# A residual load moved to a second queue, and the last stores rearranged, in a 3x3 convolution with residual add

## Chip, cores, metric

One core of one Trainium2 chip (trn2). The metric is device time in microseconds (us), lower is better. A run counts as slow when it is over 1.5% above the fastest of its kernel. One profile is one execution: sizes read from a single profile are sizes of that execution.

## Reference

```python
# x: 16 x 64 x 64 x 64, weight: 64 x 64 x 3 x 3, residual: 16 x 64 x 64 x 64, all float32
x_pad = np.pad(x, ((0, 0), (0, 0), (1, 1), (1, 1)), mode='constant')
for b, co, ci, kh, kw in ...:          # five loops
    output[b, co] += weight[co, ci, kh, kw] * x_pad[b, ci, kh:kh+h, kw:kw+w]
return (output + residual).astype(np.float32)
```

x and the residual are read once (16.8 MB each) and the output is written once (16.8 MB). With the weights that is 50.48 MB.

## The kernel before

Two images stand side by side on the 128 partitions (64 channels each) and are called a pair. There are 8 pairs. Per image, ScalarE casts x to bf16 into a padded tile, TensorE does 6 groups of 4 matmuls, and VectorE adds the result from PSUM to the residual, in place in `ro`. SyncE issues every load and store. `xr` holds three pairs of x, `ro` all eight pairs.

```python
RES = (slice(0, 1), slice(1, 2), slice(2, 4), slice(4, 6), slice(6, 8))   # residual loads, in pairs

def load_x(p):
    return nc.sync.dma_start(out=xr[p % NXR][:, :], in_=x_bc[128 * p : 128 * p + 128, :]).then_inc(s_x[p % NXR], 16)
def load_ro(i):
    if i >= 2:
        nc.sync.wait_ge(s_r[i % 2], 16 * (i // 2))
    nc.sync.dma_start(out=ro[:, RES[i], :], in_=res_bc[:, RES[i], :]).then_inc(s_r[i % 2], 16)
def store(pairs):
    return nc.sync.dma_start(out=out_bc[:, pairs, :], in_=ro[:, pairs, :])

# SyncE's program
for p in range(NPAIR):
    if p >= NXR:
        nc.sync.wait_ge(s_half, 2 * (p - NXR) + 3)     # buffer read, ScalarE's next cast done
    if p == 0:
        to_the_front(load_x(p))                        # ahead of the opening barrier
        nc.sync.dma_start(out=wraw[:, :], in_=w_rows[:, :]).then_inc(s_w, 16)
    else:
        load_x(p)
    if p in (0, 1, 3, 5, 7):
        load_ro((p + 1) // 2)
for k in range(NEARLY):                                # NEARLY = 3: pairs 0-1, 2-3, 4-5
    nc.sync.wait_ge(s_add, 4 * k + 5)
    store(slice(2 * k, 2 * k + 2)).then_inc(s_out, 16)
# ... ScalarE, VectorE and TensorE programs cut ...
for p in range(2 * NEARLY, NPAIR):                     # after all engines are done: pairs 6 and 7
    store(slice(p, p + 1))
```

Of the kernel before, what the change touches and what calls it, by code (L numbers as in the profile page):

```python
# [15 lines left out]
def kernel(  # L16
# [7 lines left out]
    nc = tc.nc  # L24
# [6 lines left out]
    NPIX = H * W  # L31
    NPAIR = B // 2
# [3 lines left out]
    NXR = 3  # L36
    NXP = 4
    NZERO = 4 + 2 * NXP
    NEARLY = 3
    RES = (slice(0, 1), slice(1, 2), slice(2, 4), slice(4, 6), slice(6, 8))  # L40

    res_bc = residual.rearrange("(p b) c h w -> (b c) p (h w)", b=2)
    out_bc = out.rearrange("(p b) c h w -> (b c) p (h w)", b=2)
# [7 lines left out]
    ro = pool.tile([128, NPAIR, NPIX], FP32)  # L51
# [10 lines left out]
    s_r = [sem(f"s_r{i}") for i in range(2)]  # L62
    s_out = sem("s_out")
# [5 lines left out]
    s_add = sem("s_add")  # L69

    def load_x(p):
        return nc.sync.dma_start(out=xr[p % NXR][:, :], in_=x_bc[128 * p : 128 * p + 128, :]).then_inc(s_x[p % NXR], 16)

    def load_ro(i):
        if i >= 2:
            nc.sync.wait_ge(s_r[i % 2], 16 * (i // 2))
        nc.sync.dma_start(out=ro[:, RES[i], :], in_=res_bc[:, RES[i], :]).then_inc(s_r[i % 2], 16)

    def store(pairs):
        return nc.sync.dma_start(out=out_bc[:, pairs, :], in_=ro[:, pairs, :])  # L80

    def matmul(out_, lhsT, rhs, start, stop, ldweights):

# [18 lines left out]
    def to_the_front(dma):  # L102



        def fixed(ap):
            t = ap.bass_ap.tensor.name
            return mybir.PhysicalAccessPattern(
                ap=ap.ap, offset=ap.bass_ap.offset, dtype=ap.dtype, memref=t, memsetref=t + "_set", bass_ap=ap.bass_ap
            )  # L110

        front = nc.main_func.blocks[0].instructions
        here = nc.cur_bb.bb.instructions
        ins = here.pop()
        assert ins.name == dma.ins.name
        at = next(
            i for i, e in enumerate(front) if e.engine == ins.engine and isinstance(e, mybir.InstDrain)
        )
        front.insert(at, copy.replace(ins, ins=[fixed(a) for a in ins.ins], outs=[fixed(a) for a in ins.outs]))
# [5 lines left out]
    def weight_block(h, half, d, par, kh):  # L125

        at = 64 * half + 32 * h
        return dict(out=wl[at : at + 32, d, :, par, :], in_=tp[0:32, kh, 0:384].rearrange("p (kw co h) -> p kw co h", kw=3, h=2)[:, :, :, h])

    with tc.tile_critical(no_gpsimd_drain=True):  # L130

        for p in range(NPAIR):
            if p >= NXR:

                nc.sync.wait_ge(s_half, 2 * (p - NXR) + 3)
            if p == 0:
                to_the_front(load_x(p))
                nc.sync.dma_start(out=wraw[:, :], in_=w_rows[:, :]).then_inc(s_w, 16)
            else:
                load_x(p)  # L140
            if p in (0, 1, 3, 5, 7):
                load_ro((p + 1) // 2)
        for k in range(NEARLY):
            nc.sync.wait_ge(s_add, 4 * k + 5)
            store(slice(2 * k, 2 * k + 2)).then_inc(s_out, 16)


        nc.gpsimd.memset(ident[:, :], 0.0).then_inc(s_id, 1)  # L148
# [2 lines left out]
            out=ident[:, :],  # L151
            in_=ident[:, :],
# [11 lines left out]
        nc.gpsimd.memset(wl[64:128, 1, :, 0, :], 0.0).then_inc(s_id, 1)  # L164


        for n in range(B):
            p, im = divmod(n, 2)
            hp = slice(64 * im, 64 * im + 64)
            x4 = xr[p % NXR].rearrange("q (j two w) -> q j two w", two=2, w=W)  # L170
            t = xp[n % NXP]
            if im == 0:
                nc.scalar.wait_ge(s_x[p % NXR], 16 * (p // NXR + 1))
            i = nc.scalar.copy(out=t[64:128, 0:J, :], in_=x4[hp, :, 0, :])  # L174
            i.then_inc(s_half, 1)
            if n >= NXP:
                i._wait_ge(s_conv, n - NXP + 1)
            nc.scalar.copy(out=t[0:64, 1 : J + 1, :], in_=x4[hp, :, 1, :]).then_inc(s_pack, 1)  # L178
            if n == 0:
                nc.scalar.wait_ge(s_id, NZERO + 1)  # L180
                for b in blocks[4:]:
                    for h in range(2):
                        i = nc.scalar.copy(**weight_block(h, *b))  # L183
                i.then_inc(s_id, 1)
# [3 lines left out]
        for k, b in enumerate(blocks[:4]):  # L188
            for h in range(2):
                i = nc.vector.tensor_copy(**weight_block(h, *b))  # L190
# [3 lines left out]
        for n in range(B):  # L194
            p, im = divmod(n, 2)
# [3 lines left out]
            if im == 0:  # L199
                i = next(i for i, pairs in enumerate(RES) if p < pairs.stop)  # L200
                nc.vector.wait_ge(s_r[i % 2], 16 * (i // 2 + 1))
            for par in range(2):
                i = nc.vector.tensor_tensor(  # L203
                    out=o4[hp, :, par, :], in0=psj[64 * par : 64 * par + 64, :, :], in1=o4[hp, :, par, :], op=ADD
                )
# [9 lines left out]
        for t in range(9):  # L215
            i = nc.tensor.transpose(  # L216
                out=tp[0:32, t // 3, 128 * (t % 3) : 128 * (t % 3) + 128], in_=wraw3[:, :, t], identity=ident[:, :]
            )
# [19 lines left out]
                m.then_inc(s_conv, 1)  # L238


    for p in range(2 * NEARLY, NPAIR):
        store(slice(p, p + 1))
    with tc.tile_critical(sync_engine=mybir.EngineType.Pool, no_gpsimd_drain=True):
        nc.gpsimd.wait_ge(s_out, 16 * NEARLY)
        tc.free_semaphores([s_w, *s_x, *s_r, s_out, s_id, s_half, s_pack, s_bank, s_conv, s_add])


# [28 lines left out]
```

## Time and profile before

| | kernel before |
|---|---|
| time, median (4 runs in the first comparison) | 122.81 us (122.63 to 122.95) |
| span of the profiled run | 120.8 us (122.68 us measured) |
| bytes moved, mean rate | 50.48 MB, 418 GB/s |
| first cast of x / first convolution / end of the last add | 7.79 / 13.78 / 104.28 us |
| last data packet ends | 119.6 us |

Two of the costliest groups of the page follow: the line and engine, what it writes and reads, the count, then busy time and mean ns of one, then the idle time of the engine just before them with what ended most of it.

```profile
L203 DVE TENSOR_TENSOR ro<-ps,ro 64x2048 f32<-64x2048 f32 x32 | 73.2, 2289 | 17.7 <-PE ps L87 17.2
...
L174 ACT CAST xp<-xr 64x2048 bf16<-64x2048 f32 x16 | 30.3, 1896 | 18.3 <-DMA xr<-in_x_dram 17.2
```

Both engines have slack: VectorE waits 17.7 us, almost wholly for TensorE, and ScalarE 18.3 us, almost wholly for x. Neither wait is what a reader should attack, because the DMA queue is full all the time (its packets took 98.5% of the 16 engines' span). The prediction below shows the lines for that.

Two quantities run through this document. They are worked out from the trace's record of single DMA packets (one packet is one row: 16 KB took 0.611 us in the middle of every run here, in the kernel before 2985 of 3072 rows; 8 KB is counted as half of that, 0.306). The **head** is the time that packets starting in the first 6 us took above those durations, summed and divided by 16 engines. In the profile before, the head is 1.04 us. The trace does not name a packet's engine. Each transfer of 64 rows or more leaves 16 packets of 4 bytes behind its rows. They are taken here as one per engine, and their times as where the transfer ends on each engine.

### The profile page before, as it was taken

What the parts mean: (1) busy time and instruction counts of PE and PEld (TensorE: products, weight loads), DVE (VectorE), ACT (ScalarE), POOL (GpSimd) and SP (SyncE); (2) the same over time, 40 slices, a digit from 0 to 9 for tenths busy, and PEclk for the clock granted to TensorE, in tenths of its full rate; (3) what the DMA queues carried; (4) which work ended last, traced back from release to release, by engine and by line L of the source; (5) the groups of instructions that cost most, each with busy time, mean ns of one, the idle gap of its engine ahead of it and who ended that gap; (6) DMA issues with size and microseconds to landing.
All of it is one profiled execution on the core that took longest, in us unless ns stands there. A gap on an engine that the chain in (4) does not pass through costs nothing.

```text
span 120.8 us, 734 instructions
## 1 busy us (share of the span) xinstructions
PE 87.9 (73%) x393; PEld 10.7 (9%) x105; DVE 76.0 (63%) x40; ACT 63.1 (52%) x37; POOL 2.4 (2%) x16
## 2 busy tenths in 40 slices
PE   0024499999999999999999999999999990000000
PEld 0011001101010011011111111011111100000000
DVE  0005400789898988989879898988989879500000
ACT  4049959948999923999960999883000000000000
POOL 5200000000000000000000000000000000000000
PEclk9999999999999999999999999999999999855555
DMA  7999999999999999999999999999999999999994
GB/s 168 428 428 428 428 428 434 428 434 434 428 434 434 434 428 434 434 434 434 434 434 423 423 428 434 423 412 434 434 434 434 423 434 434 434 428 434 434 434 174
DMA packets 3504, 50.48 MB, mean 418 GB/s; under 512 B 304, under 2 KB 432, under 8 KB 432
## 3 DMA queue, kind: packets, MB, share of 16 engines
q1 hardware_dynamic: 3504, 50.48, 98.5%
HBM read 33.70 MB, written 16.78 MB: 418 GB/s over the span
## 4 chain that ended last, share of the span: by engine, by line
PE 71%; DVEq 2%; DVE 2%; issue 0%
PE ps L87 53%; PE ps L86 18%; DVEq L130 2%; DVE ro L203 2%
## 5 line engine op out<-in xcount | busy, mean ns | idle before, releaser
L203 DVE TENSOR_TENSOR ro<-ps,ro 64x2048 f32<-64x2048 f32 x32 | 73.2, 2289 | 17.7 <-PE ps L87 17.2
L87 PE MATMUL ps<-xp,wl 128*128 128x504 bf16 (+1 forms) x288 | 80.0, 388 | 0.0
L86 PE MATMUL ps<-xp,wl 128*128 128x504 bf16 (+1 forms) x96 | 37.4, 389 | 3.4 <-PEq L224 3.4
L174 ACT CAST xp<-xr 64x2048 bf16<-64x2048 f32 x16 | 30.3, 1896 | 18.3 <-DMA xr<-in_x_dram 17.2
L178 ACT CAST xp<-xr 64x2048 bf16<-64x2048 f32 x16 | 30.4, 1897 | 0.4
L86 PEld LDWEIGHTS ps<-xp,wl 128*128 128x128 bf16 x96 | 9.5, 99 | 79.1 <-issue 79.1
L190 DVE CAST wl<-ps 32x192 bf16<-32x192 f32 x8 | 2.8, 348 | 10.6 <-PE ps L216 10.5
L216 PE MATMUL ps<-ident,wraw 128*32 128x128 f32 x9 | 2.1, 413 | 8.3 <-DMA wraw<-in_weight_dram 8.3
L216 PEld LDWEIGHTS ps<-ident,wraw 128*32 128x32 f32 x9 | 1.2, 137 | 8.7 <-issue 8.2
L174 ACT ACT_TABLE_LOAD x1 | 1.3, 1283 | 1.0 <-SPq L130 1.0
L183 ACT CAST wl<-ps 32x192 bf16<-32x192 f32 x4 | 1.2, 306 | 0.0
L162 POOL MEMSET xp<- 64x64 bf16 x4 | 0.6, 147 | 0.2
L161 POOL MEMSET xp<- 64x64 bf16 x4 | 0.6, 145 | 0.2
L150 POOL TENSOR_SCALAR_AFFINE_SELECT ident<-ident 128x128 f32<-128x128 f32 x1 | 0.3, 294 | 0.2 <-POOL ident L148 0.2
L164 POOL MEMSET wl<- 64x192 bf16 x1 | 0.3, 253 | 0.1
L163 POOL MEMSET wl<- 64x192 bf16 x1 | 0.3, 252 | 0.1
L148 POOL MEMSET ident<- 128x128 f32 x1 | 0.2, 205 | 0.6 <-SPq L130 0.6
L260 POOL MEMSET const-bfloat16-1.0<- 128x1 bf16 x1 | 0.1, 112 | 0.0
L260 POOL MEMSET const-uint8-127<- 128x1 uint8 x1 | 0.1, 112 | 0.0
L260 POOL MEMSET const-float32-0.0<- 128x1 f32 x1 | 0.1, 105 | 0.2 <-issue 0.2
L260 POOL MEMSET const-float32-1.0<- 128x1 f32 x1 | 0.1, 109 | 0.0
## 6 DMA issues: line engine op xcount, KB each, us to landing
xr<-in_x_dram SPq DMA_DIRECT2D x8, 2048.0 KB, 15.3
ro<-in_residual_dram SPq DMA_DIRECT2D x3, 4096.0 KB, 24.0
out_dram<-ro SPq DMA_DIRECT2D x3, 4096.0 KB, 33.2
ro<-in_residual_dram SPq DMA_DIRECT2D x2, 2048.0 KB, 15.9
out_dram<-ro SPq DMA_DIRECT2D x2, 2048.0 KB, 12.8
wraw<-in_weight_dram SPq DMA_DIRECT2D x1, 144.0 KB, 7.1
```

What stands on the lines that cost most here:

```text
L86: return e.matmul(out=out_, lhsT=lhsT, rhs=rhs, start=start, stop=stop, skip_group_check=True)
L87: return e.add_instruction(mybir.InstMatmult(name=nc.get_next_instruction_name(), engine=PE, ins=[e.lower_ap(rhs), e.lower_ap(lhsT)], outs ...
L130: with tc.tile_critical(no_gpsimd_drain=True):
L161: nc.gpsimd.memset(t[0:64, 0, :], 0.0).then_inc(s_id, 1)
L162: nc.gpsimd.memset(t[64:128, J, :], 0.0).then_inc(s_id, 1)
L174: i = nc.scalar.copy(out=t[64:128, 0:J, :], in_=x4[hp, :, 0, :])
L178: nc.scalar.copy(out=t[0:64, 1 : J + 1, :], in_=x4[hp, :, 1, :]).then_inc(s_pack, 1)
L183: i = nc.scalar.copy(**weight_block(h, *b))
L190: i = nc.vector.tensor_copy(**weight_block(h, *b))
L203: i = nc.vector.tensor_tensor(out=o4[hp, :, par, :], in0=psj[64 * par : 64 * par + 64, :, :], in1=o4[hp, :, par, :], op=ADD)
L216: i = nc.tensor.transpose(out=tp[0:32, t // 3, 128 * (t % 3) : 128 * (t % 3) + 128], in_=wraw3[:, :, t], identity=ident[:, :])
L260: nc = _bacc.Bacc("TRN2", target_bir_lowering=False, num_devices=1)
```

## The change

The intent: start the first residual load at once on ScalarE's own queue instead of third on SyncE's, so that the DMA engines have more to do from the start, and leave fewer bytes for after the last add: pair 6 is stored as soon as it is ready, and pair 7 in two halves.

```diff
-    NEARLY = 3
+    EARLY = (slice(0, 2), slice(2, 4), slice(4, 6), slice(6, 7))
-    def load_ro(i):
+    def load_ro(i, e):                     # body: nc.sync becomes e, and the dma is returned
-    def store(pairs):
-        return nc.sync.dma_start(out=out_bc[:, pairs, :], in_=ro[:, pairs, :])
+    def store(pairs, cols=slice(0, NPIX)):
+        return nc.sync.dma_start(out=out_bc[:, pairs, cols], in_=ro[:, pairs, cols])
-            if p in (0, 1, 3, 5, 7):
-                load_ro((p + 1) // 2)
-        for k in range(NEARLY):
-            nc.sync.wait_ge(s_add, 4 * k + 5)
-            store(slice(2 * k, 2 * k + 2)).then_inc(s_out, 16)
+            if p in (1, 3, 5, 7):
+                load_ro((p + 1) // 2, nc.sync)
+        for pairs in EARLY:
+            nc.sync.wait_ge(s_add, 2 * pairs.stop + 1)
+            store(pairs).then_inc(s_out, 16)
+        to_the_front(load_ro(0, nc.scalar))          # ahead of ScalarE's opening barrier
-    for p in range(2 * NEARLY, NPAIR):
-        store(slice(p, p + 1))
+    for h in range(2):
+        store(slice(NPAIR - 1, NPAIR), slice(NPIX // 2 * h, NPIX // 2 * (h + 1)))
-        nc.gpsimd.wait_ge(s_out, 16 * NEARLY)
+        nc.gpsimd.wait_ge(s_out, 16 * len(EARLY))
```

More of the change, by code (lines that the diff above doesn't have):

```diff
@@ L72, in load_x @@
         return nc.sync.dma_start(out=xr[p % NXR][:, :], in_=x_bc[128 * p : 128 * p + 128, :]).then_inc(s_x[p % NXR], 16)
-    def load_ro(i):
+    def load_ro(i, e):
         if i >= 2:
-            nc.sync.wait_ge(s_r[i % 2], 16 * (i // 2))
-        nc.sync.dma_start(out=ro[:, RES[i], :], in_=res_bc[:, RES[i], :]).then_inc(s_r[i % 2], 16)
-    def store(pairs):
-        return nc.sync.dma_start(out=out_bc[:, pairs, :], in_=ro[:, pairs, :])
+            e.wait_ge(s_r[i % 2], 16 * (i // 2))
+        return e.dma_start(out=ro[:, RES[i], :], in_=res_bc[:, RES[i], :]).then_inc(s_r[i % 2], 16)
+    def store(pairs, cols=slice(0, NPIX)):
+        return nc.sync.dma_start(out=out_bc[:, pairs, cols], in_=ro[:, pairs, cols])
     def matmul(out_, lhsT, rhs, start, stop, ldweights):
```

## The prediction

> **What bounds the kernel now.** I read the page first, for the row of DMA rates, then the chain of waits, then SyncE's own timeline and the short stretches at both ends.
>
> ```profile
> span 120.8 us, 734 instructions
> DMA  7999999999999999999999999999999999999994
> GB/s 168 428 428 428 428 428 434 428 434 434 428 434 434 434 428 434 434 434 434 434 434 423 423 428 434 423 412 434 434 434 434 423 434 434 434 428 434 434 434 174
> DMA packets 3504, 50.48 MB, mean 418 GB/s; under 512 B 304, under 2 KB 432, under 8 KB 432
> PE 71%; DVEq 2%; DVE 2%; issue 0%
> ```
>
> The span is cut into 40 slices of 3.02 us. Apart from the first and last slice, the 16 DMA engines are busy in all of them at 412 to 434 GB/s. The chain that ended last names TensorE (71%), but a chain is followed through instructions, and the bytes still waiting in a DMA queue are not instructions. VectorE's last add ends at 104.28 us, yet the span ends at 120.8: the 16 us after it are stores draining. So the bound is bytes: 50.48 MB at 430 GB/s is 117.4 us, plus a head and a tail. The only other way to lose time is to let the queue run empty.
>
> The stretches at the ends (columns: length, busy PE, PEld, DVE, ACT, POOL, PE clock, DMA share, GB/s):
>
> ```profile
> 0.50:1.00 0.50, 0.00 (x0) 0.00 (x0) 0.00 (x0) 0.04 (x1) 0.00 (x1) 1.00 0.00 0
> 1.00:1.50 0.50, 0.00 (x0) 0.00 (x0) 0.00 (x0) 0.50 (x1) 0.27 (x2) 1.00 2.87 524
> 1.50:2.00 0.50, 0.00 (x0) 0.00 (x0) 0.00 (x0) 0.50 (x1) 0.39 (x3) 1.00 0.38 66
> 2.00:2.50 0.50, 0.00 (x0) 0.00 (x0) 0.00 (x0) 0.24 (x1) 0.39 (x3) 1.00 0.38 98
> 2.50:3.00 0.50, 0.00 (x0) 0.00 (x0) 0.00 (x0) 0.00 (x0) 0.34 (x4) 1.00 0.77 328
> ...
> 119.00:119.50 0.50, 0.00 (x0) 0.00 (x0) 0.00 (x0) 0.00 (x0) 0.00 (x0) 0.50 0.09 33
> 119.50:120.00 0.50, 0.00 (x0) 0.00 (x0) 0.00 (x0) 0.00 (x0) 0.00 (x0) 0.50 0.00 0
> ```
>
> A packet is booked where it starts. The first 16 start just after 1.00 (share 2.87 in half a microsecond: each takes long), the second ones only by 2.5 to 3.0. The records of single packets say the same: a row of 16 KB takes 0.611 us on one engine throughout, but the first 20 take 0.7 to 2.0 us, together an excess of 16.2 us, 1.0 us per engine. By 3.00 us (524+66+98+328) x 0.5 = 508 KB have started, worth 1.17 us at 434 GB/s: it is as if full rate began at 1.83 us. The last packet starts by 119.1 and ends at 119.6; the other 1.2 us to 120.8 are completion and the end of the program. The measured time is 1.9 us more than the span (122.68 for the profiled run).
>
> SyncE's timeline and waits give the spare time of the queue:
>
> ```profile
> 1.00 0.33 SPq L138 DMA_DIRECT2D wraw<-in_weight_dram  x1
> 1.38 0.57 SPq L77 DMA_DIRECT2D ro<-in_residual_dram  x1
> ...
> 3.05 17.09 SPq L72 DMA_DIRECT2D xr<-in_x_dram  x2
> 20.18 0.43 SPq L77 DMA_DIRECT2D ro<-in_residual_dram  x1
> ...
> 57.63 47.93 SPq L80 DMA_DIRECT2D out_dram<-ro  x5
> ```
> ```profile
> SPq L72 <- ACT xp L174: 50.9, 5, 16.3
> SPq L80 <- DVE ro L203: 27.9, 2, 20.3
> SPq L130 <- DVEq L130: 17.4, 1, 17.4
> ```
>
> SyncE waits long, but always with bytes behind it. A pair of 2.10 MB takes 4.88 us at 430 GB/s. Before the fourth x load, 10.63 MB stand in the queue, enough until 1.83 + 24.7 = 26.5 us; the load is issued at 19.8: **6.7 us spare**. The last two stores are issued at 104.58; the queue ahead of them ends at 119.1 - 2 x 4.88 = 109.3: **4.7 us spare**. The stops between have more (11 us at the fifth x load).
>
> [...]
>
> **The change, part by part.** The order of instructions shows one load moved from SyncE's sixth place to ahead of ScalarE's opening barrier, one store of 4096 columns moved before the end of the critical part, and the last store cut in two of 2048. TensorE, VectorE and GpSimd keep their order. No byte is added or removed.
>
> 1. *Residual pair 0 at ScalarE's front.* ScalarE's first record in the trace (a drain) is at 0.125 us, so its load is issued at about 0.13 to 0.55, beside SyncE's first x load. SyncE saves one issue of 0.57 us, at a time when 4.9 us of x are already queued: worth nothing. The DMA engines have work from 1.0 us in both kernels. What can be won is the excess of 1.0 us per engine, if a second ring's packets fill it. Against that, engines whose first packet was quick (0.72) had a slow second one (1.77): until about 3.4 us everything is slow, whichever packet it is. So I expect a fifth to a third of it: -0.25 us.
>
> 2. *What that delays.* Taking turns, x pair 0 and residual pair 0 end together, after 4.19 MB: 1.83 + 9.76 = 11.6 us instead of 6.7. Pair 0 of x was usable at 7.79, so now at about 12.1 to 12.7; the weights, behind x, at 13.1 instead of 8.27. TensorE's transposes wait for the weights, and its first convolution came 5.5 us after them (13.78): now near 18.6, **4.8 us later**. TensorE never stalls later (16 images, 5.19 us each), so the lateness stays: the last add ends at 104.28 + 4.8 = 109.1. On the way ScalarE's third image begins at 12.1 + 3.8 (first image) + 1.3 (weights) + 3.8 (second) = 21.0, and the fourth x load is issued at about 23.0 instead of 19.8: the spare falls from 6.7 to 3.5 us, no hole. ScalarE waited 4.1 us for data twice further on (ahead of 47.17 and 66.64), so its lateness is gone there.
>
> 3. *Pair 6 stored early.* Its store is issued after image 14's first add: 94.49 + 2.29 + 4.8 = 101.6, behind a queue that lasts to 109.3: no hole, and 4.88 us more for the end. The last store comes at 109.4; the queue lasts to 119.1 - 4.88 = 114.2: 4.8 us spare. Without this part both stores would come at 109.4, with the queue out at 109.3 and about 1 us from issue to first byte: a hole of 1.1 us. So this part gives nothing itself; it pays for part 1.
>
> 4. *The last pair in two halves.* Packets of 8 KB instead of 16 KB. Program-loading packets of 8192 bytes took 0.307 us at best, half of 0.611, so no cost per packet. A finer last packet may even out the ends of the engines (119.1 to 119.6): at most 0.3 us, I put 0.05.
>
> Sum: 122.76 - 0.25 - 0.05 + 0 = 122.46, say **122.5 us**.
>
> **The rivals.** *(a) The second ring fills the whole head.* If slow starting is a latency of each ring that two rings overlap, the excess of 1.0 us vanishes: 121.7. For it: SyncE's later loads show no such excess, so it belongs to starting. Against: the slow second packets. *(b) The delay opens a hole.* If x is held back more than fair turns do, for instance because the weights take turns with what is left of the residual (8 rows of weights per engine, each behind a packet of 0.611, 4.9 us), the lateness grows from 4.8 to some 9 us and both spares of 3.5 and 4.8 come near zero: 0 to 2 us lost, 122.5 to 124.5. Against it: both loads have 8 rows per engine and start within 0.2 us, so little residual is left when the weights' turn comes. *(c) Two rings or small packets cost rate.* If 0.5% were lost in the first 10 us and the last 5, it is under 0.1 us. *(d) The rings do not alternate* and x goes first: then TensorE is late by less or not at all, and the time is still the queue's, 122.5. In all of these the end is set by bytes.
>
> **Range and chances.** The three runs before differ by 0.23 us. Rival (a) sets the low end at 121.7; a start made slower by two rings, or a short hole, the high end at 123.1. Faster by over 2% means under 120.3: more than the whole head excess, 2%. Slower by over 2% means over 125.2: a hole of 2.7 us that my spares rule out, 1.5%. The rest, 96.5%, is within 2%.
>
> **What would show each step.** Right: DMA rates of 412 to 434 in all middle slices; the first cast of xr near 12 us, the transposes near 13, the first convolution near 18.6; the last add ending near 109; five stores' worth of bytes ending near 119. Part 1 shows in the first slice (168 GB/s before) alone. Wrong: a middle slice well under 400 GB/s, most likely near 25 us or near 110; or a first convolution still near 13.8, which would say that the rings do not share. The prediction is wrong by more than its range if the head gives over 1 us or a hole appears.

That two loads on two queues take turns, as part 2 has it, was the assumption then, since the kernel before uses one queue. In the kernel after, SyncE's and ScalarE's queues each start 64 rows between 2.65 and 7.50 us. The recorded texts say "ring" for such a queue (q1, SyncE's, and q10, ScalarE's, on the pages).

## The result, and the profile after

The changed kernel takes 122.88 us (median of 4 runs, 122.74 to 123.01), the kernel before 122.81 us in the same rounds: a ratio of 1.0006, with a 95% interval of 0.9988 to 1.0024. Ratios here are the mean time of one kernel's fast runs over that of the other's of the same rounds, so they are not quite the ratio of the medians. The two kernels take the same time.

The page of the kernel after: span, DMA busy tenths and rate in 40 slices of 3.03 us, and one row of DMA issues (count, KB each, us from issue to landing).

```profile
span 121.2 us, 735 instructions
DMA  7999999999999999999999999999999999999994
GB/s 232 416 427 438 433 433 433 427 433 433 433 427 433 427 433 433 433 433 433 433 433 433 433 422 427 384 378 433 433 427 427 433 427 433 433 427 433 416 430 181
...
wraw<-in_weight_dram SPq DMA_DIRECT2D x1, 144.0 KB, 11.4
```

The first slice rose from 168 to 232 GB/s, as intended. Between the first and the last, all slices have 416 GB/s or more but two: the 26th and 27th, at 384 and 378 GB/s (76 to 82 us), where the kernel before has 423 and 412. The weights land 11.4 us after their issue instead of 7.1.

The stretches of the start and the end of the kernel after (columns as in the prediction: the last two are DMA share and GB/s):

```profile
1.00:1.50 0.50, 0.00 (x0) 0.00 (x0) 0.00 (x0) 0.43 (x1) 0.20 (x1) 1.00 2.14 492
1.50:2.00 0.50, 0.00 (x0) 0.00 (x0) 0.00 (x0) 0.50 (x1) 0.40 (x2) 1.00 0.19 66
2.00:2.50 0.50, 0.00 (x0) 0.00 (x0) 0.00 (x0) 0.35 (x1) 0.34 (x4) 1.00 0.94 393
2.50:3.00 0.50, 0.00 (x0) 0.00 (x0) 0.00 (x0) 0.00 (x0) 0.39 (x3) 1.00 0.87 360
...
119.00:119.50 0.50, 0.00 (x0) 0.00 (x0) 0.00 (x0) 0.00 (x0) 0.00 (x0) 0.50 0.82 344
119.50:120.00 0.50, 0.00 (x0) 0.00 (x0) 0.00 (x0) 0.00 (x0) 0.00 (x0) 0.50 0.13 49
```

From 2.0 to 2.5 us the rate is 393 GB/s where it was 98. At the end, packets still start between 119.5 and 120.0.

The timeline of the kernel after, at the start (start, duration, engine and line, what it does, idle time before with its releaser):

```profile
0.00 0.39 SPq L72 DMA_DIRECT2D xr<-in_x_dram  x1
0.12 0.36 ACTq L77 DMA_DIRECT2D ro<-in_residual_dram  x1
...
11.55 1.90 ACT L175 CAST xp<-xr 64x2048 bf16<-64x2048 f32 x1 [9.20 <-DMA xr<-in_x_dram]
12.62 2.08 PE L217 MATMUL ps<-ident,wraw 128*32 128x128 f32 x9 [12.62 <-DMA wraw<-in_weight_dram]
...
18.13 0.58 PE L86 MATMUL ps<-xp,wl 128*128 128x512 bf16 x1 [3.44 <-PEq L225]
```

The two first loads are issued 0.12 us apart. x is usable at 11.55 us (before: 7.79), the weights at 12.62 (8.27), and the first convolution starts at 18.13 (13.78): everything is some 4 us later, as the prediction had it for two loads in turns. This costs nothing here: the DMA tenths stay at 9 from the second slice to the last but one, since the bytes are still in the queue.

Now the place that nobody had named. The kernel before, 77 to 80 us:

```profile
77.00:78.00 1.00, 1.00 (x6) 0.10 (x1) 1.00 (x1) 1.00 (x1) 0.00 (x0) 1.00 1.01 426
78.00:79.00 1.00, 1.00 (x7) 0.10 (x1) 0.42 (x2) 0.22 (x2) 0.00 (x0) 1.00 0.96 393
79.00:80.00 1.00, 1.00 (x6) 0.10 (x1) 1.00 (x1) 1.00 (x1) 0.00 (x0) 1.00 1.09 442
```

and the kernel after:

```profile
77.00:78.00 1.00, 1.00 (x7) 0.10 (x2) 1.00 (x1) 1.00 (x1) 0.00 (x0) 1.00 0.84 328
78.00:79.00 1.00, 1.00 (x6) 0.19 (x2) 0.97 (x2) 0.97 (x2) 0.00 (x0) 1.00 1.09 262
79.00:80.00 1.00, 1.00 (x7) 0.10 (x1) 1.00 (x1) 1.00 (x1) 0.00 (x0) 1.00 1.01 377
```

The DMA share stays near 1 (the engines are not starved), but they begin 328, 262 and 377 GB/s worth of packets in these three stretches, against 426, 393 and 442. In the records, the 16 packets that start between 78.0 and 78.5 us take 0.76 to 1.36 us instead of 0.611. These packets belong to the last residual load, some four rows ahead of the first store on each engine.

The accounts of the two profiles, in us per DMA engine:

| | before | after | difference |
|---|---|---|---|
| mean start of an engine's first packet | 1.13 | 1.23 | +0.10 |
| head | 1.04 | 0.55 | -0.49 |
| slow spell | 0.12 | 0.71 | +0.59 |
| excess of packets after 90 us | 0.01 | 0.06 | +0.05 |
| mean end of an engine | 119.36 | 119.63 | +0.27 |
| end of the last engine | 119.62 | 119.98 | +0.36 |
| span | 120.85 | 121.22 | +0.37 |

The four rows above the mean end add up to +0.25, which accounts for its +0.27. So the gain of the head is real in this pair of profiles, and it is lost again 76 us later. The experiments ask whether the loss is chance, what causes it, and what each part of the change does alone.

### The profile page after: what moved, and what is told of

The parts are those of the page before. It is cut to its first block, busy times and chain, and to the rows that moved or that the text cites. A ratio compares the mean times of both kernels' runs of the same rounds, so it can differ in the third digit from the quotient of the medians.

```text
span 121.2 us, 735 instructions
## 1 busy us (share of the span) xinstructions
PE 86.5 (71%) x393; PEld 10.6 (9%) x105; DVE 76.0 (63%) x40; ACT 63.1 (52%) x37; POOL 2.4 (2%) x16
## 4 chain that ended last, share of the span: by engine, by line
PE 70%; DVEq 2%; DVE 2%; issue 0%
PE ps L87 52%; PE ps L86 18%; DVEq L130 2%; DVE ro L204 2%
## 5 line engine op out<-in xcount | busy, mean ns | idle before, releaser
L87 PE MATMUL ps<-xp,wl 128*128 128x504 bf16 (+1 forms) x288 | 78.9, 383 | 0.0
L86 PE MATMUL ps<-xp,wl 128*128 128x504 bf16 (+1 forms) x96 | 36.9, 384 | 3.4 <-PEq L225 3.4
L217 PEld LDWEIGHTS ps<-ident,wraw 128*32 128x32 f32 x9 | 1.2, 137 | 13.1 <-issue 12.6
## 6 DMA issues: line engine op xcount, KB each, us to landing
ro<-in_residual_dram ACTq DMA_DIRECT2D x1, 2048.0 KB, 12.1
out_dram<-ro SPq DMA_DIRECT2D x2, 1024.0 KB, 11.4
wraw<-in_weight_dram SPq DMA_DIRECT2D x1, 144.0 KB, 11.4
```

The costliest lines, as they stand in the source:

```text
L86: return e.matmul(out=out_, lhsT=lhsT, rhs=rhs, start=start, stop=stop, skip_group_check=True)
L87: return e.add_instruction(mybir.InstMatmult(name=nc.get_next_instruction_name(), engine=PE, ins=[e.lower_ap(rhs), e.lower_ap(lhsT)], outs ...
L217: i = nc.tensor.transpose(out=tp[0:32, t // 3, 128 * (t % 3) : 128 * (t % 3) + 128], in_=wraw3[:, :, t], identity=ident[:, :])
```

## The experiments

All were correct. Times are medians with the ratio to the kernel before in the same rounds and its 95% interval.

**r1, r2: both kernels again.** No edit. Is the spell chance?

> The kernel before, unchanged, for a second profile and for the noise of five rounds. In its first profile the first packets of the 16 DMA engines cost 1.04 us per engine more than 0.611 us each (the head), and packets near 77 to 79 us cost 0.12 us (the slow spell). Theory A (the head is shorter in the changed kernel for good; the slow spell is chance and ate the gain in one profile): head again near 1.0, slow spell anywhere from 0.1 to 0.7. Theory B (the change itself lengthens the slow spell): slow spell again 0.1 to 0.2. Theory C (both sizes are chance): head anywhere from 0.5 to 1.1. Ratio to before 0.999 to 1.001 in all.

> The changed kernel, unchanged. Its first profile had a head of 0.55 us and a slow spell of 0.71 us per engine. Theory A: head near 0.55 again, slow spell anywhere from 0.1 to 0.7, so that over five rounds the time is 0.2 to 0.4 us under the kernel before (ratio 0.997 to 0.998). Theory B: head near 0.55, slow spell near 0.7 again, ratio 1.000 to 1.002. Theory C: head and slow spell both wander, ratio 0.999 to 1.001.

r1: 122.83 us (ratio to itself 1.0007, 0.9992 to 1.0021, which is the noise). Head 0.81, spell 0.03. r2: 122.95 us (1.0010, 0.9997 to 1.0023). Head 0.50, spell 0.66. The changed kernel has the spell again and the kernel before has not. Theory A (chance) falls. The spell comes with the change.

**r3: the front part alone.** After, with the stores of before:

```diff
-    EARLY = (slice(0, 2), slice(2, 4), slice(4, 6), slice(6, 7))
+    EARLY = (slice(0, 2), slice(2, 4), slice(4, 6))
-    for h in range(2):
-        store(slice(NPAIR - 1, NPAIR), slice(NPIX // 2 * h, NPIX // 2 * (h + 1)))
+    for p in range(NPAIR - 2, NPAIR):
+        store(slice(p, p + 1))
```

> Only the residual at the front of ScalarE's program; pairs 6 and 7 are stored whole after the last add, as before. My prediction said that this alone would open a hole of 1.1 us before the last two stores, worked out with a last add 4.8 us later; in the profile after, the last add ended only 2.9 us later (107.2 against 104.3). If the prediction's account holds with the lateness of 4.8: 1.1 us slower than the changed kernel, and a slice under 400 GB/s near 109 us. With the measured lateness of 2.9: the stores are issued near 107.5, the queue lasts to 109.8 and a first byte takes 1 us, so no hole: same as the changed kernel within 0.2 us. If the slow spell of 0.7 belongs to the front part it shows here too.

122.93 us (1.0006, 0.9993 to 1.0019), the same as r2 (122.95). Head 0.51, spell 0.70. The last add ends at 108.67 us, later than I expected here (107.2), and the two stores are issued at 108.96. A hole does open; the stretch of r3 where it shows is:

```profile
110.00:111.00 1.00, 0.00 (x0) 0.00 (x0) 0.00 (x0) 0.00 (x0) 0.00 (x0) 0.50 0.70 295
```

The store ahead of these two ends on the first engine at 109.55 us and on the last at 110.09. The next store, normally 4.86 us of work, ends 5.16 us later on the first engine and 4.90 us later on the last. So the hole is 0.30 us for the engine that was earliest and 0.04 us for the one that was latest, and the latest sets the end. With r4, which follows, this puts the spell down to the front part.

**r4: the stores alone.** After, with the loads of before:

```diff
-            if p in (1, 3, 5, 7):
+            if p in (0, 1, 3, 5, 7):
-        to_the_front(load_ro(0, nc.scalar))
```

> Only the stores of the change: pair 6 early, pair 7 in two halves; the loads as in the kernel before. All theories: no hole, last add near 104.3, same as before within 0.1 us; if the halves cost or give something at the end, the last packets end 0.05 to 0.3 us away from 119.6. Theory B in its form that the front part lengthens the slow spell: 0.1 to 0.2 here; in its form that the stores do: 0.6 to 0.7 here.

123.00 us (1.0013, 1.0001 to 1.0025): same at 2%, if anything 0.15 us longer. Head 0.74, spell 0.15. The engines end within 0.80 us of one another (before 0.50, r1 0.71), so the halves do not even out the ends, and packets after 90 us cost 0.06 us. The stores give nothing and do not make the spell. The rates of r3 (first row) and r4 (second), in 40 slices, show it in the 26th and 27th: 373 and 384 against 427 and 433.

```profile
GB/s 249 428 433 411 433 433 433 433 433 433 428 433 433 433 433 433 428 433 433 433 428 433 433 433 422 373 384 433 433 428 428 433 428 433 433 428 417 433 433 173
GB/s 173 433 406 433 433 433 433 433 433 433 433 433 433 433 433 433 433 433 433 427 433 433 433 427 433 427 433 427 433 433 433 433 422 433 422 433 433 400 427 157
```

**r5: engines put out of step.** After, with two small loads behind the weights, whose bytes the last load brings again:

```diff
                 nc.sync.dma_start(out=wraw[:, :], in_=w_rows[:, :]).then_inc(s_w, 16)
+                for rows, cols in ((slice(0, 8), slice(0, 2048)), (slice(0, 4), slice(2048, 4096))):
+                    nc.sync.dma_start(out=ro[rows, 7, cols], in_=res_bc[rows, 7, cols]).then_inc(s_d, 16)
...
+                if p == 7:
+                    nc.sync.wait_ge(s_d, 32)
                 load_ro((p + 1) // 2, nc.sync)
```

> The changed kernel with the engines put out of step: right behind the weights, two small loads of 8 KB rows of residual pair 7[...], which the last load brings once more after waiting for them. In the six profiles so far the 16 engines finished one and the same mid-kernel load within 0.79 to 1.02 us of one another with the old front (slow spell at 77 to 80 us: 0.03 to 0.15 us per engine) and within 0.35 to 0.59 us with the new front (slow spell 0.66 to 0.71). Theory L (engines in step all turn from loads to stores together, and that is slow): spread about 0.9 to 1.1 us, slow spell down to 0.05 to 0.3. Theory R (having used a second ring makes the spell): spell stays 0.6 to 0.7. Theory M (the later ScalarE and TensorE make it): stays 0.6 to 0.7. Time: under L about as the kernel before, 122.7 to 123.1; under R and M 0.3 to 0.6 us longer than the changed kernel, 123.2 to 123.5.

124.26 us (1.0105, 1.0088 to 1.0122), well over what any theory said. Head 0.57, spell at the turn at most 0.02, and the engines are 1.31 us apart both ahead of the turn and at the end. But another slow stretch appeared where the small loads run: 1.44 us per engine between 8 and 16 us, mostly in the packets of the x load behind them. All the 96 KB go to partitions 0 to 7; the two small loads have 12 closing packets (8 + 4), so, taken as one per engine, they gave extra work to some engines and none to the others. Which engines these were was not shown. So the spell did vanish, as theory L said, but not cleanly: the small loads brought a stall of their own that may have changed something else.

**r6: a second queue for the weights only.** Before, with

```diff
-                nc.sync.dma_start(out=wraw[:, :], in_=w_rows[:, :]).then_inc(s_w, 16)
+                nc.scalar.dma_start(out=wraw[:, :], in_=w_rows[:, :]).then_inc(s_w, 16)
```

> The kernel before with nothing changed but that the weights (0.15 MB) go by ScalarE's queue, issued after the opening barrier. So a second ring is used, and no x is delayed by more than 0.2 us. Theory L: head and spread decide; if the head stays near 0.8 to 1.0 and the spread near 0.8 to 1.0, the slow spell stays at 0.03 to 0.2. Theory R: slow spell 0.6 to 0.7. Theory M: 0.03 to 0.2. Time within 0.2 us of before in all but R (0.4 longer).

122.90 us (1.0001, 0.9984 to 1.0017). Head 0.84, spell 0.06. Theory R (any use of a second queue) falls. The engines stood within 0.62 us of one another before the turn, and 15 of the 16 within 0.30 us. By theory L such engines should have had a long spell. That speaks against L as well.

**r7: the first store ahead of the last load.** After, with

```diff
+            if p == 7:
+                nc.sync.wait_ge(s_add, 2 * EARLY[0].stop + 1)
+                store(EARLY[0]).then_inc(s_out, 16)
             if p in (1, 3, 5, 7):
                 load_ro((p + 1) // 2, nc.sync)
-        for pairs in EARLY:
+        for pairs in EARLY[1:]:
```

> The changed kernel with the first double store moved ahead of the last double load of residual in SyncE's program: loads turn to stores some 9.7 us sooner, near 70 us, back to loads near 80 and to stores again near 90. If the slow spell belongs to the turn from loads to stores: excess of 0.5 to 0.7 us per engine in packets near 67 to 70 us, and none of that size at 77 to 80; a second spell near 87 to 90, smaller if the first one has changed the steps of the engines. If it belongs to a time since the start (something outside the program): again at 77 to 80. Time 0 to 0.6 us longer than the changed kernel.

123.13 us (1.0017, 1.0000 to 1.0034). Head 0.58. The spell moved with the first store (stretches of r7):

```profile
68.00:70.00 2.00, 2.00 (x11) 0.20 (x2) 1.97 (x2) 1.98 (x2) 0.00 (x0) 1.00 0.93 279
...
78.00:80.00 2.00, 2.00 (x11) 0.21 (x3) 1.97 (x2) 1.98 (x2) 0.00 (x0) 1.00 1.05 451
```

279 GB/s at 68 to 70 us, where the changed kernel has 418, and 451 at 78 to 80, where that has 319. The excess at 68 to 72 us is 0.64 us per engine. So the spell belongs to the first turn from loads to stores and not to a time. The second such turn, near 90 us, shows no excess, though the engines are within 0.51 us of one another: a second point against L.

**r8: as early, but in one queue.** Before, with the first residual load at SyncE's front:

```diff
                 to_the_front(load_x(p))
+                to_the_front(load_ro(0))        # load_ro returns its dma
...
-            if p in (0, 1, 3, 5, 7):
+            if p in (1, 3, 5, 7):
```

> The kernel before with the first residual pair at the front of SyncE's program behind the first x load: as early as in the change, but in one ring and without delay for x (first cast near 7.8 us, the first convolution near 13.8). If the shorter head (0.50 to 0.55 against 0.74 to 1.04 us) comes from the second ring, the head stays at 0.75 to 1.05 here; if from 4 MB being queued before the barrier, it is 0.5 to 0.6. Theory L: slow spell follows the spread: under 0.2 when the spread is over 0.75, 0.6 to 0.7 when it is under 0.6. Theories R and M: slow spell 0.03 to 0.2 whatever the spread. Time as before within 0.3 us.

123.05 us (1.0012, 0.9995 to 1.0028). Head 0.95, spell 0.09. Two stretches of r8:

```profile
2.00:2.50 0.50, 0.00 (x0) 0.00 (x0) 0.00 (x0) 0.50 (x1) 0.39 (x3) 1.00 0.64 164
...
78.00:80.00 2.00, 2.00 (x11) 0.20 (x2) 1.97 (x2) 1.98 (x2) 0.00 (x0) 1.00 1.01 418
```

The start is as slow as before (164 GB/s at 2.0 to 2.5 us), so having both loads queued before the barrier does not shorten the head (0.95). With the second of them on ScalarE's queue it is 0.50 to 0.58. The last add ended at 107.78 us, as late as in the changed kernel (107.22), and there is no spell: theory M (later compute) falls. That it was late I had not expected: the weights, behind the residual in the one queue, held the first convolution back to 18.70 us, where I had written 13.8.

**r9: x in two queues, cut by rows.** Before, with x pair 0 as rows 0 to 63 at SyncE's front and 64 to 127 at ScalarE's:

```diff
-                to_the_front(load_x(p))
+                for e, rows in ((nc.sync, slice(0, 64)), (nc.scalar, slice(64, 128))):
+                    to_the_front(e.dma_start(out=xr[0][rows, :], in_=x_bc[rows, :]).then_inc(s_x[0], 16))
...                                             # and ScalarE waits for 16 more on s_x[0]
```

> The kernel before with only the first x load cut in two: rows 0 to 63 at SyncE's front, rows 64 to 127 at ScalarE's front; residual and stores as before. Both rings carry 1 MB at the start and x is not delayed (first cast near 7.8 us). So far the four profiles with 2 MB of residual on the second ring at the front have a head of 0.50 to 0.58 us and, at the first turn from loads to stores, a spell of 0.64 to 0.71 (0.02 with the engines put out of step); all others have 0.74 to 1.04 and 0.03 to 0.15. Theory S (two rings in turns at the start shorten the head and leave a debt to be paid at the first stores): head 0.5 to 0.6, spell 0.6 to 0.7, time within 0.2 us of before. Theory L (engines in step): head 0.5 to 0.6 and, if the engines are then within 0.6 us, a spell of 0.6 to 0.7. If the two are separate things: head 0.5 to 0.6, spell under 0.2, time 0.3 to 0.5 us shorter than before, 122.4 to 122.6. If the head stays at 0.75 to 1.05, the shorter head needs the 4 MB of two loads.

127.18 us (1.0353, 1.0339 to 1.0366), over 4 us slower. A stretch of r9:

```profile
6.00:9.00 3.00, 0.00 (x0) 0.00 (x0) 0.00 (x0) 0.00 (x0) 0.00 (x0) 1.00 1.13 237
```

Until x is in, at 10.7 to 11.6 us, the rate is about half: a row takes 1.25 us (median) instead of 0.611, with the engines busy (DMA share 0.98 and 1.13 at 3 to 6 and 6 to 9 us). Why rows of one half of the partitions take twice as long was not shown. The records show SyncE's four rows on every engine first and ScalarE's four after them, so the halves hardly ran together: SyncE's half landed 8.5 us after its issue, ScalarE's 12.2. The run tells nothing of the head; it was repeated with columns (r12). Its engines are within 0.43 us of one another and its spell is at most 0.02, but after such a start this counts little.

**r10: turns of two queues in the middle.** Before, with the residual load of pairs 2 and 3 on ScalarE's queue:

```diff
-            if p in (0, 1, 3, 5, 7):
+            if p in (0, 1, 5, 7):
...
             i.then_inc(s_half, 1)
+            if n == 2:
+                load_ro(2, nc.scalar)
```

> The kernel before with one change in the middle: the first double load of residual (pairs 2 and 3, 4.2 MB) goes by ScalarE's queue, issued after its cast of the third image near 20 us, so two rings take turns for some 20 us of the run, while the head is that of the kernel before. Theory S in the form that it is the turns of two rings that leave a debt: head 0.75 to 1.05, spell at 77 to 80 us of 0.6 to 0.7, time 0.4 to 0.7 us longer than before. If it is only the shorter head that leaves the debt: spell 0.03 to 0.2, time as before within 0.2 us. Theory L: spell follows the spread of the engines before the turn: over 0.6 us if that is under 0.6.

123.89 us (1.0056, 1.0027 to 1.0086), in two groups: four runs at 123.88 to 123.99, two at 122.92 and 123.06. In the profile (a run of 123.95) the head is 0.89 and the spell 0.35, half a spell, unevenly spread: the last engine ends the load ahead at 71.17 us and the last load at 82.00, which is 1.1 us more than the usual 9.72. So one engine fell behind at the turn itself; the last ends at 120.88 us while the mean end is 119.70 (before: 119.62 and 119.36). The result lies between the two outcomes that I had written down, and I leave it as unclear.

**r11: ScalarE's issue after the barrier.** After, with

```diff
-        to_the_front(load_ro(0, nc.scalar))
+        load_ro(0, nc.scalar)
```

> The changed kernel, but ScalarE issues residual pair 0 after the opening barrier (near 1.0 us) instead of ahead of it. The rings still take turns over the same two loads, only the second ring comes in about 0.9 us later. If the shorter head comes from the early issue: head 0.75 to 1.05; if from the turns: 0.5 to 0.6. If the turns leave the spell behind: 0.6 to 0.7 us per engine at 77 to 80 us whatever the head, and with a long head the time is 0.3 to 0.5 us longer than the changed kernel (123.2 to 123.4). If only the shorter head leaves it behind: long head and spell under 0.2, time as before, 122.7 to 122.9. The last add ends 2.5 to 5 us later than before in any case, without cost.

122.96 us (1.0005, 0.9991 to 1.0019). Head 0.84, spell 0.13. ScalarE issued at 0.96 us instead of 0.12. Two stretches of r11:

```profile
2.00:2.50 0.50, 0.00 (x0) 0.00 (x0) 0.00 (x0) 0.50 (x1) 0.39 (x3) 1.00 0.59 164
...
78.00:80.00 2.00, 2.00 (x11) 0.29 (x3) 1.42 (x2) 1.41 (x1) 0.00 (x0) 1.00 0.97 393
```

Rows of the two queues still mix, if for a shorter time: x pair 0 ends on the engines at 8.26 to 9.90 us (before 6.44 to 7.21, after 10.57 to 11.18). At 0.611 us a row I estimate from these ends that three or four rows of residual came ahead of its last row, where in the changed kernel it was about seven. There is neither the short head nor the spell. So three or four turns did not leave a spell behind here. In the profiles so far short head and spell go together, but for r5 (short head, no spell) and r10 (long head, half a spell).

**r12: x in two queues, cut by columns.** r9 with

```diff
-                for e, rows in ((nc.sync, slice(0, 64)), (nc.scalar, slice(64, 128))):
-                    to_the_front(e.dma_start(out=xr[0][rows, :], in_=x_bc[rows, :]).then_inc(s_x[0], 16))
+                for e, cols in ((nc.sync, slice(0, 2048)), (nc.scalar, slice(2048, 4096))):
+                    to_the_front(e.dma_start(out=xr[0][:, cols], in_=x_bc[0:128, cols]).then_inc(s_x[0], 16))
```

> The repair of the run that cut x by rows (64 partitions at a time ran at half the rate, so it told nothing of the head): x pair 0 cut by columns, 128 partitions and 1 MB on each ring, both at the front; residual on SyncE's queue. 8 KB packets at 0.306 us. x is not delayed: first cast near 7.8 us. If two rings at the start shorten the head: 0.5 to 0.6. If the short head always leaves the spell behind: 0.6 to 0.7 at 77 to 80 us and time as before; if the spell belongs to the residual in turns with x: under 0.2, and time 122.3 to 122.6, faster than both kernels. If the head is 0.75 to 1.05: time as before, spell under 0.2.

122.98 us (1.0014, 1.0001 to 1.0028). First cast at 7.85 us, head 0.73, spell 0.18. The head is not shortened clearly (0.69 with its 8 KB packets counted at 0.309; r4 has 0.74 without any second queue), though both queues were in use from the front, so an early second queue alone is not shown to be enough, and the time is not better. No version here beats both kernels.

**All profiles side by side**, in us per engine (left out: r5 and r9, which brought stalls of their own, and r10, which stayed unclear):

| front | head | spell | mean end | last end |
|---|---|---|---|---|
| residual at ScalarE's front: after, r2, r3, r7 | 0.50 to 0.58 | 0.64 to 0.71 | 119.52 to 119.66 | 119.83 to 119.98 |
| all others: before, r1, r4, r6, r8, r11, r12 | 0.73 to 1.04 | 0.03 to 0.18 | 119.24 to 119.38 | 119.62 to 119.94 |

The two rows do not overlap in head or in spell. The mean of the last ends is 119.89 in the first row and 119.76 in the second: 0.13 us apart, about the 0.1 us by which the changed kernel's median exceeds that of before. The mean ends are 0.28 us apart (119.60 and 119.32), but with the short head the engines end closer together, which gives half of it back.

## Why the prediction was right or wrong

The time (122.88 against 122.5, range 121.7 to 123.1): right. "Same" follows from the bound on bytes. That the time came so near is partly luck: the forecast gain of 0.3 us did not come, because a gain at the head larger than I put met a loss that I had not put at all. Step by step:

- **The bound: right.** Bytes set the end: the DMA packets took 98.5% of the 16 engines' span in the kernel before and 98.4% in the one after. TensorE began 4.35 us later, and the time did not move (ratio 1.0006). r8, with the last add 3.5 us later, says the same.
- **Part 1, the head: right in sign, wrong in its cause, too small.** I put a gain of 0.25 us, from a second queue's packets that fill the slow start. The first pair of profiles gives 0.49, the means of the table's two groups about 0.53 and 0.85, so 0.32. But ScalarE's packets fill nothing: on each engine they come third, from 2.65 us on (all 31 packets that start before are SyncE's), and it is SyncE's own first two packets that run faster (0.61 to 1.48 us and then mostly 0.611, where before they took up to 2.03 and four of the second ones 1.1 to 1.8). The gain was not there without the second queue (r8, head 0.95) nor without the early issue (r11, 0.84); r12, with both and x cut by columns, has no clearly shorter head (0.73). Why a load that has not yet moved a packet makes those of the other queue faster stays open.
- **The step that was missing: the spell.** "Sum: 122.76 - 0.25 - 0.05 + 0" has no term for the place where loads give way to stores. It costs 0.59 us more than before in the first profiles, more than the head gives. I named lateness at 25 us and 110 us as the danger and treated the middle as untouched. Shown: it comes with the front part (r3 against r4), it belongs to the first turn from loads to stores (r7), it is not chance (four of four profiles with the changed front, r5 with its extra loads apart), it does not come from a second queue as such (r6 0.06, r12 0.18), nor from three or four turns with the first (r11, 0.13), nor from later compute (r8, 0.09). So "the only other way to lose time is to let the queue run empty" failed: here the engines were busy. It went with the short head in all but r5 and r10. That turns of two queues in the middle make part of it is not excluded (r10: 0.35 with a head of 0.89). Engines in step (theory L) fit most profiles, but r6 and the second turn of r7 speak against it. The mechanism stays open.
- **Part 2, the delay: right, with one wrong sentence.** First cast 11.55 (predicted 12.1 to 12.7), weights 12.62 (13.1), first convolution 18.13 (18.6), x in turns with the residual as assumed (in the trace of the kernel after from the third packet on: 64 rows of each queue start between 2.65 and 7.50 us). The fourth x load stands just ahead of the issue at 22.70 (23.0). "TensorE never stalls later, so the lateness stays" failed in the profile after: the last add ended 2.9 us late instead of 4.8, since TensorE's slow first matmuls (a group of four in about 1.7 us instead of 0.87) lasted until 20.9, 2.8 us from its start, where before they lasted 5.3 us. In r2 and r3 the last adds ended at 108.61 and 108.67, 4.3 and 4.4 us late. So this length varies between runs, and it costs nothing.
- **Part 3, pair 6 early: right that it gives nothing, wrong that it is needed.** The hole without it was put at 1.1 us; r3 shows 0.30 us on the earliest engine, 0.04 on the latest, and no time. The terms that were mis-sized: the queue ahead ended at 109.55 to 110.09 and not at 109.3 (I counted back from 119.1, where the last packet starts, instead of 119.6, where the last one ends; head and spell together moved its mean end only from 109.63 to 109.79), and the stores were issued at 108.96 and not at 109.4.
- **Part 4, halves: wrong in sign, tiny.** Expected -0.05; they cost about 0.05, and the ends of the engines are not evened out. "So no cost per packet" failed: an 8 KB packet of the stores took 0.309 us, not half of 0.611, and each engine has 16 of them.
- **The rivals.** (a), the whole head filled, did not happen: half of it remained. (b), a hole from lateness, did not happen. (c), a loss of rate by two queues or small packets in the first 10 and the last 5 us, was too small to matter (packets after 90 us: 0.05 us more than before). None of them was the spell. My sign of error "a middle slice well under 400 GB/s" did show (378), but not where I looked, and with the engines busy.

## What to carry to other kernels

Here the DMA queue was full from start to end, and moving a load earlier or to another queue only changed the order of bytes: six such versions (r2, r3, r6, r8, r11, r12) have ratios of 1.0001 to 1.0014 (r10, with a load moved in the middle, has 1.0056 and stayed unclear). In such a kernel look instead at what the engines lose at the start (head, 0.50 to 1.04 us in the table), at the first turn from loads to stores (spell, 0.03 to 0.71) and by not ending together (0.50 us in the kernel before, 0.80 in r4), and sum these over the packet records before believing in a faster first slice. A gain seen in one slice of a profile has to be followed to the end of the span. Do not cut a bulk load by partition halves to use two queues without measuring it: r9, which did, took 4.4 us more than the kernel before.
